# A gated decoder layer on one core: weights' low parts on VectorE, channel means in other banks, a new order of the gate jobs

## The chip, the cores and the metric

The kernel runs on one core of a Trainium2 chip. The metric is the device time of one execution in microseconds; the time given for a kernel is the median of its runs. One more execution was taken by the hardware profiler, and all rows below are from it.

## The reference

One decoder layer on a sequence of 1024 tokens and 1024 channels, in float32. With h the RMS-normalized input, one projection gives the parts of three branches and their gates:

```python
(c_glu, c_gate, d_q, d_k, d_v, d_gate, x_q, x_gate, merge) = split(h @ w_in)
# A: u = a * sigmoid(b); causal depthwise conv (k = 31) + bias; LayerNorm over channels; silu; * silu(c_gate); @ w_conv_proj
# B: differential attention, 8 heads of 2 x 64, ALiBi, RMS-normalized q and k; * silu(d_gate); @ w_diff_proj
# C: attention into 256 memory tokens, 4 heads of 256; * silu(x_gate); @ w_x_proj
g = sigmoid(merge)
x = x + (g[0] * y_conv + g[1] * y_diff + g[2] * y_mem) @ w_out
```

The LayerNorm of branch A needs the mean and the variance of the convolution's output over all 1024 channels. The kernel has channels on partitions, so these are sums over eight channel blocks and, in each, over the 128 partitions.

## The kernel before

**Numbers as two parts.** A matrix product in full precision is made of three matmuls of reduced-precision float32: each operand x is cut into a high part H (a cast on ScalarE) and a low part L = x - H (a subtraction on VectorE or GpSimd). `split` (L82) does both.

**Stages.** First the memory tokens, the norm of x, the first half of the GLU and the cross attention. Then, from L558 on, the Quads stage, which the change edits: the rest of the projection of h. Then the differential attention with the branch projections woven in, and last the output projection.

**Quads jobs.** In the Quads stage two blocks of 128 output channels are one job. A job is a two-by-two Strassen-like product (`strassen`, L629): seven products p1 to p7 of 12 matmuls each (128x128 weights, 512 moving columns), so 84 matmuls. The right-hand sides are quarters of h (tiles `hH`, `hL`) and the sums T1 to T4 of them, which `sums` (L580) makes once, at the start of the stage: for each of four k, GpSimd adds H and L of three quarters into tiles (`whole`, L572), VectorE subtracts these from each other, and `split` cuts the results. The left-hand sides are sums of quarters of the weights: `Quads.__call__` (L603) loads four raw tiles (two with tag "wraw", two with tag "wraw2" of 4 slots), GpSimd makes four sums of them (L621; s1 and s2 go to tag "ws" of 2 slots), ScalarE casts seven high parts (L623), and seven low parts follow (L624), some on GpSimd (`on_pool`) and the others on VectorE. The weights of a job are asked for in the middle of the job before.

The products of a job run into three accumulator banks, "tp" (tag a), "mm" (b) and "sc" (d). ScalarE copies a bank out between the products that it gathers (`snap`, L647, the "snap" of the text), VectorE adds (L650). The products p7, p3 and p4 of one job alternate with p1, p5 and p6 of the next, and with two "tp" banks the first product of a job needs the last snap of the bank two jobs back, which is taken only one product (2.7 us) earlier.

**The 38 jobs, in order:** 0 and 1 GLU, 2 to 5 merge gates, 6 and 7 GLU, 8 to 13 merge gates, 14 to 17 the cross-attention gate (`gx_out`, L740), then plain jobs (their output is only an activation and a store: the attention gate and v), and the convolution's gate (`gc_out`, L838); from job 28 on query/key jobs (`qk_out`, L755) with two more v jobs. While jobs 0 to 15 run, VectorE has the depthwise convolution to do (`conv`, L414, low priority: 31 instructions for each half block).

**The statistics.** `part_stats` (L802) brings each finished block back from memory and updates a running mean and deviation for each partition. After job 17 (MU_AT) `colmean` (L927) averages the mean over the 128 partitions by two matmuls with a matrix of 1/1024 for each half of the sequence (L931); after job 19 (RS_AT) the same for the deviation, followed by the chain `rstd_of` (L167: Ln, Exp and a Newton step) in place. `colsplit` (L919) cuts the operands one job earlier. `gate_in` (L818) later loads each block again and normalizes it: a - mean (L833), times dev (L834), Silu (L836).

**Order.** Only TensorE's order is that of the program. On the other engines and on SP, which issues all the DMAs, a scheduler with a timeline of its own orders the instructions by priority and estimated readiness; each engine then works in that order, and an instruction that waits holds all behind it. Tiles of one tag share its slots: a new tile waits until the one that had its slot is done with.

Of the kernel before, what the change touches and what calls it, by code (L numbers as in the profile page):

```python
# [10 lines left out]
F32R = mybir.dt.float32r  # L11
# [4 lines left out]
P = 128  # L16
S = 1024
# [13 lines left out]
def hybrid_layer(  # L31
# [36 lines left out]
    def new(pool, shape, tag, dt=F32, bufs=None):  # L68
        return pool.tile(shape, dt, tag=tag, name=tag, bufs=bufs)

    def r2f(ap):
        return ap.bitcast(F32)

    def mm_bank(tag="mm"):
        return banks[tag].tile([P, 512], F32, tag=tag, name=tag)
# [6 lines left out]
    def split(H, L, src):  # L82
        nc.scalar.copy(H, src)  # L83
        nc.vector.tensor_tensor(L, src, r2f(H), op=ALU.subtract)  # L84
# [5 lines left out]
    class Weights:  # L90


        def __init__(self, rows, width=512, low=None, high=None, ks=range(KK)):
            self.ks = ks
            self.raw = lambda kk: new(wp, [P, 512], "wraw", bufs=4)
            self.high = high or (lambda kk: nc.scalar.copy)
            self.rows, self.width, self.low, self.slices = rows, width, low or (lambda kk: nc.vector), None
# [106 lines left out]
    def halves():  # L204
        return [(half, slice(half * 512, half * 512 + 512)) for half in range(2)]
# [22 lines left out]
    with ExitStack() as st:  # L228
# [145 lines left out]
        for n in range(8):  # L374
# [10 lines left out]
            u = (m_u[1] if n == 0 else []) + x_u[n]  # L385
# [16 lines left out]
    cvp = cvs.enter_context(tc.tile_pool(name="cvp", bufs=2, side="right", reuse_waits="tile"))  # L402
    with ExitStack() as st:
        bp = st.enter_context(tc.tile_pool(name="bp", bufs=2, reuse_waits="tile"))
# [153 lines left out]
    with ExitStack() as st:  # L558
        bp = st.enter_context(tc.tile_pool(name="b2", bufs=2, reuse_waits="tile"))
# [12 lines left out]
        def whole(q, k, tag, bufs):  # L572
            t = new(bp, [P, 512], tag, bufs=bufs)
            H, L = quad[q](k)
            nc.gpsimd.tensor_tensor(t, r2f(H), r2f(L), op=ALU.add)
            return t
# [2 lines left out]

        def sums():  # L580
            for k in range(4):
                b11, b12 = whole("B11", k, "wraw2", 4), whole("B12", k, "wraw2", 4)
                b22 = whole("B22", k, "wraw2", 4)
                nc.vector.tensor_tensor(b11, b12, b11, op=ALU.subtract)
                split(*quad["T1"](k), b11)
                nc.vector.tensor_tensor(b12, b22, b12, op=ALU.subtract)
                split(*quad["T3"](k), b12)
                nc.vector.tensor_tensor(b22, b22, b11, op=ALU.subtract)
                split(*quad["T2"](k), b22)
                t4.append(whole("B21", k, "w4", 4))  # L590
                nc.vector.tensor_tensor(t4[k], t4[k], b22, op=ALU.subtract)
# [5 lines left out]
        class Quads:  # L597


            def __init__(self, c1, c2):  # L600
                self.c, self.ops, self.busy = (c1, c2), None, False

            def __call__(self):  # L603
                if self.ops is None:
                    raw = []
                    for i in range(2):
                        for j in range(2):
                            t = new(wp, [P, 512], "wraw", bufs=4) if i == 0 else new(bp, [P, 512], "wraw2", bufs=4)
                            c = self.c[i]
                            nc.sync.dma_start(t.rearrange("p (k c) -> p k c", k=4),  # L610
                                              w0[j * 512:j * 512 + 512, c:c + P].rearrange("(k p) c -> p k c", p=P))
                            raw.append(t)
                    a11, a12, a21, a22 = raw
                    s1, s2 = [new(bp, [P, 512], "ws", bufs=2) for _ in range(2)]
                    sums = {0: ((s1, a21, a22, ALU.add), (s2, s1, a11, ALU.subtract), (a21, a11, a21, ALU.subtract)),
                            6: ((a12, a12, s2, ALU.subtract),)}
                    on_pool = (1, 3, 4, 5, 6) if self.busy else (1, 3, 4, 6)
                    ops = {}
                    for n, a in ((0, a11), (1, s1), (2, s2), (3, a12), (4, a21), (6, a22), (5, a12)):
                        for o, x, y, op in sums.get(n, ()):  # L620
                            nc.gpsimd.tensor_tensor(o, x, y, op=op)  # L621
                        H, L = new(wp, [P, 512], "wH", F32R), new(wp, [P, 512], "wL", F32R)
                        nc.scalar.copy(H, a)  # L623
                        (nc.gpsimd if n in on_pool else nc.vector).tensor_tensor(L, a, r2f(H), op=ALU.subtract)  # L624
                        ops[n] = H, L
                    self.ops = [ops[n] for n in range(7)]
                return self.ops
# [162 lines left out]
        def spill(n, dst, c0, func=AF.Sigmoid):  # L790
            return [(Quads(c0 + n * 512 + p * 256, c0 + n * 512 + p * 256 + P), spill_out(dst, n * 512 + p * 256, func))
                    for p in range(2)]

        def glus(c2):
            return [(Quads(c2 * 256 + p * P, D + c2 * 256 + p * P), glu_out(2 * c2 + p)) for p in range(2)]
# [42 lines left out]
        def gc_out(c):  # L838
# [12 lines left out]
            return f  # L851

        sums()
        jobs = glus(2) + spill(2, sgT, C_MERGE) + spill(3, sgT, C_MERGE) + glus(3)
        for n in (4, 5, 1):
            jobs += spill(n, sgT, C_MERGE)
        def v_job(v):
            c = C_Q + 2 * D + v * 256
            return Quads(c, c + P), spill_out(vT[v], 0, None)
# [3 lines left out]
        def start(n, at, f):  # L863
            starts.setdefault((n, at), []).append(f)

        plain = spill(0, gdT, C_DGATE, AF.Silu) + spill(1, gdT, C_DGATE, AF.Silu) + [v_job(0), v_job(1)]
        for c in range(0, KK, 2):
            n = len(jobs)
            for (i, j), late, at in (((0, 0), 0, 3), ((1, 1), 0, 5), ((0, 1), 1, 0), ((1, 0), 1, 2)):
                start(n + late, at, gx_in(c + i, j))  # L870
            jobs.append((Quads(C_XGATE + c * P, C_XGATE + c * P + P), gx_out(c)))
        jobs += plain[:3]
        for c in range(0, KK, 2):
            for at, (i, j) in enumerate(((0, 0), (1, 1), (0, 1), (1, 0))):
                start(len(jobs) - 1, at, gate_in(c + i, j))
            jobs.append((Quads(C_GATE + c * P, C_GATE + c * P + P), gc_out(c)))
            jobs += plain[3:4]
            del plain[3:4]
        V_AT = {4: [2], 7: [3]}
        for h in range(DH):  # L880
            jobs.append((Quads(C_Q + h * P, C_Q + D + h * P), qk_out(h), True))
# [5 lines left out]
        def stats(n):  # L887

            if n == 1:
                nc.vector.memset(r2f(ones), 1.0 / D)  # L890
                nc.sync.dma_start(mean, cvT[0:P, :])
            if n in (MU_AT - 1, RS_AT - 1):
                with tc.issue_after(last[0].ins):
                    stat["cs"] = colsplit(mean if n < MU_AT else dev)
            if n == MU_AT:
                for half, sl in halves():
                    ps = colmean(half)
                    d = new(bp, [P, 512], "w4", bufs=4)
                    nc.vector.scalar_tensor_tensor(d, ps, -8.0, mean[:, sl], op0=ALU.mult, op1=ALU.add)
                    nc.scalar.activation(mean[:, sl], ps, AF.Copy, scale=8.0)  # L900
                    nc.scalar.activation(d, d, AF.Square, scale=math.sqrt(8.0))
                    nc.vector.tensor_tensor(dev[:, sl], dev[:, sl], d, op=ALU.add)
            if n == RS_AT:
                for half, sl in halves():
                    nc.scalar.copy(dev[:, sl], colmean(half))
                tc.keep_in_program_order(nc.scalar.preload_act_table_set(NLE))
                for half, sl in halves():
                    rstd_of(dev[:, sl], dev[:, sl], [P, 512], 1.0, 1e-5, eps5, nc.vector, bp, ("w4", "w4"), 4)
# [8 lines left out]
                on[:] = [f for f in on if next(f, 0) is None]  # L917

        def colsplit(src):  # L919
            cs = []  # L920
            for half, sl in halves():
                H, L = new(bp, [P, 512], "w4", F32R, bufs=4), new(bp, [P, 512], "w4", F32R, bufs=4)
                split(H, L, src[:, sl])
                cs.append((H, L))
            return cs

        def colmean(half):  # L927

            ps = mm_bank()
            for n, x in enumerate(stat["cs"][half]):  # L930
                nc.tensor.matmul(ps, lhsT=ones, rhs=x, start=n == 0, stop=n == 1)  # L931
            return ps
# [9 lines left out]

        gx, gc = g_load(gxT), g_load((gcH, gcL))
        due, AFTER, last, qkp = [], 1, [None], []
        for Q, *_ in jobs[2:16]:
            Q.busy = True
        PRE, MU_AT, RS_AT = 2, 17, 19
        weave(merge(0, bp, "sx", 7, AF.Sigmoid), pre(jobs[0][0]))
        sums4()
# [32 lines left out]
    with ExitStack() as st:  # L982
# [344 lines left out]
        c = 0  # L1327
# [47 lines left out]
    with ExitStack() as st:  # L1375
# [18 lines left out]
        for ci in range(2):  # L1394
            for db in range(4):
                if db == 1:
                    Ws[ci + 1]()
                d = 4 * ci + db
# [12 lines left out]
        for ci in range(2):  # L1411
            for sb in range(NS):
                if ci == 0 and sb == 2:
                    Wp["o"][1]()
                sl = slice(sb * P, sb * P + P)
# [37 lines left out]
```

## Time and profile before

| | |
|---|---|
| time of the runs, median (lowest to highest) | 1743.38 us (1742.48 to 1743.82) |
| the profiled execution: time | 1747.11 us |
| the profiled execution: span from first to last instruction | 1745.1 us |
| busy TensorE, VectorE, ScalarE, GpSimd | 95%, 74%, 53%, 53% of the span |
| mean granted TensorE clock | 0.978 |

PE is TensorE's matmuls, PEld its weight loads, DVE VectorE, ACT ScalarE, POOL GpSimd, SP the DMA queue's engine. Times in rows are us from the span's start, unless ns is said. An arrow in square brackets names what ended an engine's idle time. The clock is a share of 2.4 GHz; 0.5 is 1.2 GHz.

### The profile page before, as it was taken

Reading aid. Unit: us, or ns where it says so; the run is one execution under the profiler, and the core shown is the slowest. Engines: PE = TensorE matmul, PEld = TensorE weight load, DVE = VectorE, ACT = ScalarE, POOL = GpSimd, SP = SyncE. Lnnn points to the kernel's source line nnn. Section 1 sums busy time; section 2 is a strip of 40 time slices with the busy share of each in tenths; the row PEclk is TensorE's granted clock in tenths of the full one; section 3 lists DMA queues with packets and bytes.
Section 4 is the critical chain, followed back from the end, with each engine's and each line's share of the span. In section 5 each row is a group of like instructions: output and inputs, shape, how many; then the busy total and the mean of one; then the engine's idle time right before and its main releaser. Section 6 shows DMA issues by size and latency. Waiting matters only on the chain. (4 is left out here: it accounts for less than half of the span.)

```text
span 1745.1 us, 24253 instructions
## 1 busy us (share of the span) xinstructions
PE 1653.5 (95%) x7882; PEld 1371.4 (79%) x7882; DVE 1285.8 (74%) x2156; ACT 919.0 (53%) x1949; POOL 925.1 (53%) x935
## 2 busy tenths in 40 slices
PE   6999999989999999798999999998997999999999
PEld 5788888868887887677888778876886878877787
DVE  7979997998999998675664896744666677675911
ACT  5614645334544444465555786843676776763200
POOL 3220111678686876555665677544456564457820
PEclk8999999989999999899999999999998999999999
DMA  7410212232432445543444333297478455466632
GB/s 264 153 36 22 77 62 76 97 103 85 133 116 90 135 145 168 174 152 108 163 160 144 97 97 109 93 334 213 135 234 262 130 167 166 140 224 202 202 115 91
DMA packets 201399, 247.51 MB, mean 142 GB/s; under 512 B 15377, under 2 KB 109590, under 8 KB 201272
## 3 DMA queue, kind: packets, MB, share of 16 engines
q1 hardware_dynamic: 201272, 245.96, 43.6%
q8 instruction: 62, 1.02, 0.2%
q14 instruction: 65, 0.53, 0.1%
HBM read 172.50 MB, written 73.40 MB: 141 GB/s over the span
## 5 line engine op out<-in xcount | busy, mean ns | idle before, releaser
L422 DVE SCALAR_TENSOR_TENSOR cv<-u,cw,cv 128x512 f32<-128x512 f32 x464 | 348.9, 752 | 10.8
L113 POOL TENSOR_TENSOR wL<-wraw,wH 128x512 fp32r<-128x512 f32 x104 | 143.0, 1390 | 255.5 <-ACT wH L112 154.8
L78 PE MATMUL mm<-hH,wH 128*128 128x512 f32 x512 | 207.6, 406 | 0.6 <-DVE sg L1194 0.6
L624 POOL TENSOR_TENSOR wL<-wraw,wH 128x512 fp32r<-128x512 f32 x128 | 185.0, 1453 | 43.3 <-ACT wH L623 37.3
L80 PE MATMUL mm<-hH,wL 128*128 128x512 f32 x512 | 202.7, 396 | 0.0
L79 PE MATMUL mm<-hL,wH 128*128 128x512 f32 x512 | 202.6, 396 | 0.0
L623 ACT CAST wH<-wraw 128x512 fp32r<-128x512 f32 x190 | 115.2, 617 | 105.7 <-PE tp L642 37.7
L1054 DVE CUSTOM_DVE_ANT_0 p<-sc,dist 128x512 f32<-128x512 f32 (+3 forms) x192 | 100.3, 551 | 59.9 <-PE sc L1050 59.5
L642 PE MATMUL tp<-hH,wH 128*128 128x512 f32 x304 | 122.3, 402 | 17.1 <-ACT sx L647 17.1
L624 POOL TENSOR_TENSOR wL<-ws,wH 128x512 fp32r<-128x512 f32 x38 | 51.9, 1366 | 148.7 <-ACT wH L623 141.3
L1068 ACT ACTIVATE p<-p,nm 128x768 f32<-128x768 f32 (+7 forms) x128 | 98.3, 770 | 50.0 <-DVE nm L1066 49.7
L642 PE MATMUL tp<-hL,wH 128*128 128x512 f32 x304 | 121.5, 400 | 0.0
L642 PE MATMUL tp<-hH,wL 128*128 128x512 f32 x304 | 121.4, 399 | 0.0
L80 PEld LDWEIGHTS mm<-hH,wL 128*128 128x128 f32 x512 | 97.8, 191 | 21.5
L78 PEld LDWEIGHTS mm<-hH,wH 128*128 128x128 f32 x512 | 97.9, 191 | 18.6 <-DVE sg L1194 0.8
L79 PEld LDWEIGHTS mm<-hL,wH 128*128 128x128 f32 x512 | 98.1, 192 | 17.9
L112 ACT CAST wH<-wraw 128x512 fp32r<-128x512 f32 (+1 forms) x112 | 64.5, 589 | 64.1 <-PE mm L80 33.8
L647 ACT COPY sx<-tp 128x512 f32<-128x512 f32 x152 | 88.1, 579 | 12.3 <-PE tp L642 7.1
L623 ACT CAST wH<-ws 128x512 fp32r<-128x512 f32 x76 | 47.0, 619 | 73.5 <-PE tp L642 66.9
L642 PEld LDWEIGHTS tp<-hH,wH 128*128 128x128 f32 x304 | 59.0, 194 | 32.0 <-ACT sx L647 19.7
L1048 PE MATMUL sc<-k,q 128*128 128x512 f32 (+2 forms) x192 | 70.4, 374 | 10.8 <-DVE mx L1054 10.7
L1100 PEld LDWEIGHTS av<-v,a 128*128 128x128 f32 x576 | 70.5, 191 | 9.0 <-ACT a L1094 4.0
(319 smaller groups left out, 4812.6 us busy)
## 6 DMA issues: line engine op xcount, KB each, us to landing
wraw<-in_w_in_dram SPq DMA_DIRECT2D x184, 256.0 KB, 3.3
sg<-sgT SPq DMA_DIRECT2D x65, 256.0 KB, 3.4
sgT<-sx SPq DMA_DIRECT2D x48, 256.0 KB, 3.2
qf<-qT SPq DMA_DIRECT2D x32, 256.0 KB, 4.3
kf<-kT SPq DMA_DIRECT2D x32, 256.0 KB, 4.2
yT<-sg SPq DMA_DIRECT2D x32, 256.0 KB, 3.7
w<-cvT SPq DMA_DIRECT2D x20, 256.0 KB, 2.9
mw<-in_w_mem_kv_dram SPq DMA_DIRECT2D x16, 256.0 KB, 5.7
```

Source lines behind the costliest of these rows:

```text
L78: nc.tensor.matmul(ps, lhsT=lh, rhs=rh, start=start, stop=False)
L79: nc.tensor.matmul(ps, lhsT=lh, rhs=rl, start=False, stop=False)
L80: nc.tensor.matmul(ps, lhsT=ll, rhs=rh, start=False, stop=stop)
L113: self.low(kk).tensor_tensor(L[:, :w], raw[:, :w], r2f(H[:, :w]), op=ALU.subtract)
L422: nc.vector.scalar_tensor_tensor(ps if j < CONV_K - 1 else acc, u[:, at - j:at - j + 512], cw[:, c, 30 - j:31 - j], ps, op0=ALU.mult, op1= ...
L623: nc.scalar.copy(H, a)
L624: (nc.gpsimd if n in on_pool else nc.vector).tensor_tensor(L, a, r2f(H), op=ALU.subtract)
L642: nc.tensor.matmul(R[bank], lhsT=l[:, ks], rhs=r, start=start and k == 0 and i == 0, stop=stop and k == 3 and i == 2, skip_group_check=True)
L647: last[0] = nc.scalar.copy(R[n], R[bank])
L1054: nc.vector.tensor_tensor_reduce(out=pm[m][:, k0:k0 + w], in0=sc[m][:, :w], in1=dist[:, d0:d0 + w], scale=1.0, scalar=-3.0e38, op0=ALU.add ...
L1068: nc.scalar.activation(pm[m][:, :n], pm[m][:, :n], AF.Exp, bias=nm[:, m:m + 1], scale=slope, accum_out=sm[:, m:m + 1])
L1100: nc.tensor.matmul(A["av"][:, t * P:t * P + P], lhsT=A["a", jp][:, c * P:c * P + P], rhs=T["v", j // 4][:, j % 4, :], start=j == 0 and t = ...
```

## The change

Five edits, all in the Quads stage. (1) The set of low parts that go to GpSimd: as before in jobs 0 and 1 (four) and 2 to 15 (five), but none from job 16 on, where it was four; all seven are then VectorE's. (2) In `sums`, b11 and b12 are tiles of tag "ws" in place of "wraw2". (3) `colmean` uses banks "av" and "cv" for the two halves in place of "mm" twice. (4) `colsplit` puts its parts into two full-length tiles of tag "u" (two slots, those of the convolution's input) in place of four of tag "w4" (four slots); one scratch tile of the statistics moves from "w4" to "acc". (5) Four of the plain jobs stand ahead of the first conv-gate job, where it was three. The order of jobs 18 on is then plain x 4, conv gate 0, v, conv gate 2, v, conv gate 4, conv gate 6; it was plain x 3, conv gate 0, plain, conv gate 2, v, conv gate 4, v, conv gate 6.

```diff
@@ sums
-                b11, b12 = whole("B11", k, "wraw2", 4), whole("B12", k, "wraw2", 4)
+                b11, b12 = whole("B11", k, "ws", 2), whole("B12", k, "ws", 2)
@@ Quads
-                self.c, self.ops, self.busy = (c1, c2), None, False
+                self.c, self.ops, self.stage = (c1, c2), None, "gates"
-                    on_pool = (1, 3, 4, 5, 6) if self.busy else (1, 3, 4, 6)
+                    on_pool = {"start": (1, 3, 4, 6), "conv": (1, 3, 4, 5, 6), "gates": ()}[self.stage]
@@ jobs
-        jobs += plain[:3]
+        jobs += plain[:4]
         for c in range(0, KK, 2):
...
             jobs.append((Quads(C_GATE + c * P, C_GATE + c * P + P), gc_out(c)))
-            jobs += plain[3:4]
-            del plain[3:4]
+            jobs += plain[4 + c // 2:5 + c // 2]
@@ stats
-                    d = new(bp, [P, 512], "w4", bufs=4)
+                    d = new(cvp, [P, 512], "acc")
@@
         def colsplit(src):
-            cs = []
+            H, L = [new(cvp, [P, S], "u").bitcast(F32R) for _ in range(2)]
             for half, sl in halves():
-                H, L = new(bp, [P, 512], "w4", F32R, bufs=4), new(bp, [P, 512], "w4", F32R, bufs=4)
-                split(H, L, src[:, sl])
-                cs.append((H, L))
-            return cs
+                split(H[:, sl], L[:, sl], src[:, sl])
+            return [(H[:, sl], L[:, sl]) for _, sl in halves()]
         def colmean(half):
-            ps = mm_bank()
+            ps = mm_bank(("av", "cv")[half])
@@
-        for Q, *_ in jobs[2:16]:
-            Q.busy = True
+        for n, (Q, *_) in enumerate(jobs[:16]):
+            Q.stage = "start" if n < 2 else "conv"
```

## Rows read from the trace of the kernel before

**Rows 1.** TensorE's waits, whole run: for whom, us in total, times, longest

```profile
PE tp L642 <- ACT sx L647: 24.8, 8, 6.5
...
PE mm L931 <- DVE sx L650: 5.9, 2, 5.3
...
PE av L773 <- DVE ms L84: 2.6, 4, 0.7
```

**Rows 2.** Windows cut at job starts: jobs 3, 16 to 21, 24, 31

```profile
core 0: us, PE busy (x) PEld busy (x) DVE busy (x) ACT busy (x) POOL busy (x), PEclk, DMA share, GB/s
424.00:443.00 19.00, 19.00 (x85) 15.76 (x84) 18.61 (x24) 9.48 (x17) 13.36 (x11) 1.00 0.40 125
...
676.90:702.80 25.90, 19.37 (x85) 15.71 (x85) 18.72 (x17) 11.84 (x23) 19.09 (x13) 0.97 0.68 223
702.80:731.30 28.50, 23.18 (x89) 18.67 (x90) 17.61 (x18) 12.64 (x24) 12.76 (x9) 0.86 0.44 144
731.30:753.40 22.10, 21.05 (x85) 16.89 (x83) 17.82 (x20) 11.81 (x22) 12.93 (x8) 0.91 0.54 186
753.40:774.40 21.00, 20.39 (x89) 16.57 (x90) 14.26 (x16) 12.52 (x24) 12.07 (x8) 1.00 0.44 149
774.40:799.30 24.90, 19.22 (x86) 15.58 (x84) 20.50 (x24) 18.31 (x27) 12.28 (x8) 0.95 0.35 113
799.30:820.40 21.10, 21.10 (x84) 17.30 (x85) 6.89 (x9) 10.77 (x19) 10.28 (x8) 0.90 0.42 132
...
858.50:877.60 19.10, 19.10 (x86) 15.81 (x85) 14.43 (x16) 11.95 (x21) 13.77 (x9) 1.00 0.55 181
...
998.90:1020.80 21.90, 21.26 (x93) 17.15 (x92) 19.91 (x21) 17.69 (x33) 15.86 (x10) 1.00 0.30 96
```

**Rows 3.** TensorE's timeline: the first matmul after each of four waits

```profile
377.46 0.79 PE L642 MATMUL tp<-T2H,wH 128*128 128x512 f32 x1 [6.34 <-ACT sx L647]
...
702.78 0.79 PE L642 MATMUL tp<-hH,wH 128*128 128x512 f32 x1 [6.48 <-ACT sx L647]
...
730.28 1.19 PE L931 MATMUL mm<-w,ones 128*128 128x512 f32 x2 [5.32 <-DVE sx L650]
...
799.28 0.79 PE L642 MATMUL tp<-hH,wH 128*128 128x512 f32 x1 [5.68 <-ACT sx L647]
```

**Rows 4.** ScalarE's timeline near the same waits

```profile
375.26 1.14 ACT L623 CAST wH<-wraw 128x512 fp32r<-128x512 f32 x2 [4.45 <-POOL wraw L621]
...
712.16 0.62 ACT L83 CAST w<-mean 128x512 fp32r<-128x512 f32 x1 [7.87 <-DMA gxTL<-w]
...
724.16 0.62 ACT L83 CAST w<-mean 128x512 fp32r<-128x512 f32 x1 [3.17 <-DMA gxTL<-w]
...
791.81 0.63 ACT L728 ACTIVATE sx<-sx 128x512 f32<-128x512 f32 x1 [3.61 <-DVE sx L650]
```

**Rows 5.** VectorE's timeline, jobs 16 to 20

```profile
690.51 1.76 DVE L811 SCALAR_TENSOR_TENSOR mean<-acc,mean 128x512 f32<-128x512 f32 x1 [3.30 <-POOL acc L809]
692.20 1.77 DVE L624 TENSOR_TENSOR wL<-ws,wH 128x512 fp32r<-128x512 f32 x1
...
728.14 0.79 DVE L84 TENSOR_TENSOR w<-mean,w 128x512 fp32r<-128x512 f32 x1 [2.12 <-DMA gxTL<-w]
728.85 0.68 DVE L624 TENSOR_TENSOR wL<-wraw,wH 128x512 fp32r<-128x512 f32 x1
729.45 0.68 DVE L650 TENSOR_TENSOR sx<-mm,sx 128x512 f32<-128x512 f32 x1
...
787.69 1.78 DVE L833 TENSOR_TENSOR w<-w,mean 128x512 f32<-128x512 f32 x1
```

**Rows 6.** GpSimd's timeline: first job sum of job 0; a low part

```profile
362.88 1.29 POOL L621 TENSOR_TENSOR ws<-wraw,wraw 128x512 f32<-128x512 f32 x1 [7.58 <-DMA sgT<-sx]
...
713.38 1.29 POOL L624 TENSOR_TENSOR wL<-ws,wH 128x512 fp32r<-128x512 f32 x1 [9.78 <-ACT wH L623]
```

**Rows 7.** GpSimd's groups, 676.9 to 1146: xcount | busy us, mean ns | idle before

```profile
L624 POOL TENSOR_TENSOR wL<-wraw,wH 128x512 fp32r<-128x512 f32 x64 | 98.3, 1544 | 26.9 <-ACT wH L623 20.9 <-DVE u L833 3.0 <-PE av L773 1.3
```

**Rows 8.** SP's timeline: the two loads into "wraw2" for job 0

```profile
355.87 4.14 SPq L610 DMA_DIRECT2D wraw<-in_w_in_dram  x2
```

## The prediction

> **What bounds the kernel now.** The order in which I read: the waits of TensorE over the whole run, then the windows cut at the job boundaries, then the instructions of each engine around the waits that the windows point to. TensorE's waits add up to little in the run, and the largest group is for the snap of an accumulator bank by ScalarE (L647), 24.8 us in 8 waits; two waits before the channel-mean matmuls L931 cost 5.9 us [rows 1]. In the windows the reader sees that an undisturbed Quads job (84 matmuls) takes 19.0 us, 0.226 us a matmul, with TensorE busy all of it, and that this holds even where VectorE is 98% busy with the convolution (18.61 of 19.00 us, the window at 424). So VectorE's load alone doesn't hold TensorE; a snap that stands behind a blocked instruction does. Jobs 16 to 21 (676.9 to 820.4) are longer by 6.9, 9.5, 3.1, 2.0, 5.9 and 2.1 us [rows 2]. That is 29.5 us; the eight matmuls L931 are 1.8 of it, which leaves 27.7 us of waits and of lower clock after them. I split it into five stalls by the waits [rows 3] and the granted clock [rows 2] (job 21 has no wait of its own, but a clock of 0.90, and is 2.1 us long for it, so this is the price of the 1.2 GHz level after a long stall):
>
> A, ending 702.78: 6.9 us in job 16 and some 2.5 us of low clock after it, 9.4 us. B, before the second half of the mean's L931, ending 730.28: 5.3 us, 0.8 us of low clock in job 17 and 2.0 us in job 18 (0.09 of 22.1 us), 8.1 us. C, the rest of job 18: 1.1 us. D, the second pair of L931 in job 19: 2.0 - 0.9 = 1.1 us. E, ending 799.28: 5.9 us in job 20 and 2.1 us in job 21, 8.0 us.
>
> One more stall lies in job 0: 6.3 us up to 377.46 [rows 3], and with as much low clock after it as after A about 9 us. The query/key jobs (one is the window at 998.9) take 21.9 us: 19.0, eight matmuls of the means (1.8) and 1.1 us that contains a wait for VectorE's low part L84 (2.6 us in four such waits) [rows 1, 2].
>
> **The change part by part.**
>
> *Channel means.* B is a wait for bank "mm": VectorE reads it at 729.45 for 0.68 us (L650), and TensorE goes on at 730.28 [rows 3, 5]. In banks "av" and "cv", unused at that time, this wait goes. But the bank isn't all: the low part of the same mean (L84) ran only at 728.14, 2.12 us late for a DMA that empties a "w4" tile, and ScalarE stood at its L83 for 7.87 and 3.17 us for the same reason [rows 4, 5]. The new bank alone would move the matmul from 730.28 to about 729.0, 1.3 us. Since the four "w4" tiles go too (the "u" slots are free: the convolution's last output was written before), both causes fall. The snap of the job before, behind that L83, comes earlier by the 3.17 us. I take 7.5 of B's 8.1 us, bounds 1.3 and 8.1. D has the same cause; I take 1.0. The price: gate_in's first "u" tiles now come after the second L931 (about 774), no longer long ahead. Their four loads queue on SP behind that release, and VectorE's L833 and L834 behind the loads. They are due one job after that, so I count nothing; without this cover it is one load and two subtractions, some 5 us.
>
> *Order of jobs.* Moving the fourth plain gate job ahead puts gate_in for conv channels 0 and 1 one job (19 us) behind the rstd chain of job 20, no longer beside it. E is the snap held behind the Silu at 791.81, which waited 3.61 us for VectorE's add L650, which stood behind L833 (787.69, 1.78 us) and its neighbours of the same length, the rstd product and a low part [rows 4, 5]. Without the two to four gate_in instructions there (3 to 7 us) most of E goes; the table switches of the chain stay. I take 5 of 8.0, bounds 0 and 8.0. C lies behind the same hoisted L833: 1.0, bounds 0 and 1.1. Every other DMA keeps its job; the last two gate jobs now follow each other. The heaviest gate window had 14.43 of 19.1 us on VectorE (at 858.5) [rows 2], so room is left: 0, bound a loss of 6 (1 us a job).
>
> *Low parts on VectorE.* In 22 jobs four TensorTensors move from GpSimd (1544 ns in the mean of the larger group) [rows 7] to VectorE. One takes 1.29 us there undisturbed (713.38) [rows 6]. On VectorE a low part takes 0.68 us when alone (728.85) and 1.77 while GpSimd works (692.20) [rows 5]. In a query/key job VectorE has 21 instructions and 19.9 busy us of 21.9, GpSimd ten [rows 2]. At 0.68 each the 21 need 14.3 us, so ten GpSimd instructions cost VectorE 5.6 us of waiting, 0.56 each. After: 25 x 0.68 + 6 x 0.56 = 20.4 us against 19.9. It still fits. I take 1 us gained in all, as the 1.1 us wait may shrink a little; bounds: at 1.77 each the four cost 7.1 us against 2.0 us of room, 5 us lost in each of six full jobs, 30; or the wait goes in all six, 6 gained. Queued behind a low part on VectorE that waits for ScalarE's cast are the adds L650, behind these the Silu on ScalarE, and behind that the snap. On GpSimd the first low part of a job waited 9.78 us for its cast at 713.38 [rows 6] and nobody minded.
>
> The Trainium skill, "SBUF — State Buffer", section "Who interferes with whom", has it that a VectorE instruction with two SBUF inputs and a GpSimd instruction that reads SBUF exclude each other for the whole of the first one. By this rule, with 1.29 and 0.68 us, six GpSimd instructions and 18 of VectorE that read two SBUF operands hold the port for 20.0 us of a query/key job, against 22.4 for ten and 14 before, and the sum would have 6 us here in place of 1. The trace agrees in kind (1.77 beside 0.68), but it shows waits of 0.56 us, not 1.29, for each GpSimd instruction.
>
> A is not touched by name: VectorE waited 3.30 us for GpSimd's L809 at 690.51 and then worked off a row of instructions of about 1.77 us [rows 5], ScalarE and the snap behind it. Fewer low parts on GpSimd shorten it, more on VectorE lengthen it: 0, bounds a gain of 9.4 and a loss of 4.
>
> *Sums at the start (L582).* With b11 and b12 in "ws", the second matrix's raw tiles no longer wait for the end of the sums. Now their second load is issued near 359.6, as the last subtraction of the sums ends, and GpSimd's first job sum starts at 362.88, 7.58 us idle; ScalarE's cast at 375.26 waits for a later one of these, and the snap behind it for the cast [rows 4, 6, 8]. After, the first sum needs only "ws", free at about 359.7: 3 us earlier. The two-slot "ws" lets b11 and b12 of a step start after the last one's, two GpSimd instructions as b12 and b22 are now, so the pace stays. I take 3 gained; bounds 9 gained, 2 lost.
>
> Sum: 7.5 + 1 + 5 + 1 + 1 + 3 = 18.5 us off a span of 1745.1. That execution took 1747.1 with what lies around the span, 3.7 above the median of 1743.4; the difference is carried over to the median: **1725 us**.
>
> **The rivals.**
>
> *R1, the stalls move.* The bank waits go, but the mean and rstd chains still end late, and TensorE meets ScalarE's late snap one job on. For: the snap waits (24.8 us) are four times those of the banks; the table switches stay. Against: undisturbed gate jobs of 19.0 us. Gain: 1.3 to 3 of B, 1 of D, 3 at the start: 1737.
>
> *R2, VectorE's queue becomes the bound (slower).* A moved low part blocks the in-order queue in the query/key jobs, where 2.0 us are free. For: the 91% there. Against: 98% under the convolution with no loss. At the upper bound 30 us are lost: 1743.4 - 18.5 + 30 = 1755. It decides above 2.3 us a job over the eight jobs. The Trainium skill, "Perfetto Trace Analysis", section "Optimizing Scalar/DVE Operations", advises moving work off a saturated VectorE, and adds that between it and GpSimd this might not help because they share a read port. The change goes the other way, and no row of this trace yet shows which half of that advice holds here.
>
> *R3, GpSimd's quiet also takes A and the query/key waits.* For: the row of 1.77 us instructions behind A. Against: its first cause is a load, not GpSimd. 18.5 + 9.4 x 0.8 + 5 = 31: 1712.
>
> **How the numbers follow.** The forecast has 0.53 (its own range 1717 to 1733), R1 0.20, R2 0.14, R3 0.13. About 0.2%, 3.5 us, is what a measurement can tell from no change: 1739.9 to 1746.9. R1 reaches it with 0.07 of its 0.20, R2 with 0.02 of its 0.14. Faster: 0.53 + 0.13 + 0.13 = 0.79; same 0.09; slower 0.12. A range from 1711 to 1743 leaves out R2, the far end of R1 and the lower part of R3, 0.2 together.
>
> **What would show it.** L931 in other banks with no wait over 1 us; jobs 17 to 20 at 19 to 21 us with the clock at 2.4 GHz; first job sum near 359.7; VectorE's low parts mostly at 0.68 us; query/key jobs no longer than 21.9. Wrong: query/key jobs over 24 us, a snap wait over 4 us in jobs 17 to 21, or VectorE idle behind casts while ScalarE waits for its adds.

## The result and the profile after

The changed kernel takes 1715.9 us in the median of four runs (1714.7 to 1723.8), the kernel before beside it 1743.6 us (1742.5 to 1748.3). The ratio is 0.985, with a 95% interval from 0.982 to 0.987: 27.7 us faster, where 18.5 were forecast (1725 us, range 1711 to 1743). The profiled execution took 1714.70 us with a span of 1712.9 us and a mean clock of 0.988. The changed source is three lines shorter from `colmean` on, so L931 of before is L928 now, and in the attention L1048 is L1045.

TensorE's waits, whole run, as in [rows 1]:

```profile
PE tp L642 <- ACT sx L647: 5.7, 4, 2.7
PE tp L642 <- DVE wL L624: 5.6, 2, 3.0
PE sc L642 <- POOL wL L624: 3.2, 1, 3.2
PE av L773 <- DVE ms L84: 1.8, 4, 0.5
```

The waits for the snap fell from 24.8 to 5.7 us, those at the channel means are gone. In their place are three waits for low parts, 8.8 us, all in jobs 0 and 1. The windows, cut at job starts as in [rows 2]: job 1, jobs 16 to 21, a gate job (24), a query/key job (31):

```profile
core 0: us, PE busy (x) PEld busy (x) DVE busy (x) ACT busy (x) POOL busy (x), PEclk, DMA share, GB/s
...
384.10:407.80 23.70, 20.73 (x85) 16.73 (x84) 21.35 (x21) 10.12 (x18) 23.07 (x17) 0.93 0.26 78
...
678.40:697.80 19.40, 19.38 (x85) 15.69 (x84) 19.30 (x21) 11.86 (x22) 11.47 (x8) 1.00 0.67 217
697.80:717.90 20.10, 20.08 (x88) 16.64 (x89) 19.88 (x26) 13.76 (x25) 10.38 (x5) 1.00 0.67 211
717.90:737.00 19.10, 19.10 (x86) 15.80 (x85) 17.04 (x22) 13.23 (x25) 6.61 (x4) 1.00 0.76 251
737.00:756.90 19.90, 19.90 (x89) 16.50 (x88) 11.39 (x16) 10.73 (x20) 5.50 (x4) 1.00 0.55 177
756.90:776.30 19.40, 19.29 (x86) 15.62 (x85) 16.38 (x25) 15.96 (x25) 7.60 (x4) 1.00 0.48 151
776.30:795.40 19.10, 19.10 (x84) 15.84 (x85) 16.04 (x22) 11.67 (x21) 7.92 (x5) 1.00 0.51 164
852.60:871.60 19.00, 19.00 (x85) 15.74 (x84) 14.10 (x18) 12.34 (x22) 5.82 (x4) 1.00 0.57 179
...
972.00:993.70 21.70, 21.24 (x93) 17.17 (x92) 20.21 (x25) 17.59 (x33) 9.56 (x6) 1.00 0.30 97
```

Read the lengths first: jobs 16 to 21 take 117.0 us where they took 143.5, and the clock stays at 2.4 GHz. VectorE does 25 instructions in the query/key job in place of 21, in 20.2 busy us in place of 19.9; GpSimd's part falls from 15.9 to 9.6 us. In jobs 16 and 17 VectorE is 99% busy, and TensorE waits for next to nothing.

Where the 32.2 us between the two spans went: jobs 15 to 21 give 27.1, jobs 28 to 36 give 2.6, jobs 0 and 1 lose 2.7, job 37 loses 2.1 (it takes 32.0 to 36.4 us over all these kernels, for reasons not looked for), the jobs between give 0.7, and 6.7 lie behind the last matmul of the Quads stage, where nothing was changed. That tail took 578 to 583 us in all twelve profiles of the experiments below, also where only the sums or only the banks were edited, against 586.8 in the one profile of before. So most of these 6.7 us belong to that execution and not to the change; the medians, 27.7 us apart, lie near the 25.6 that the Quads stage gave.

VectorE's timeline at the place of stall A, to be read beside [rows 5]:

```profile
686.37 0.68 DVE L811 SCALAR_TENSOR_TENSOR mean<-acc,mean 128x512 f32<-128x512 f32 x1
...
689.88 1.77 DVE L624 TENSOR_TENSOR wL<-ws,wH 128x512 fp32r<-128x512 f32 x1
691.58 0.68 DVE L650 TENSOR_TENSOR sx<-sx 128x512 f32<-128x512 f32 x1
692.19 0.68 DVE L84 TENSOR_TENSOR w<-w,sx 128x512 fp32r<-128x512 f32 x1
```

The instruction that updates the mean took 1.76 us with 3.30 us of idling before it; it takes 0.68 now, without idling. A row of five instructions of 1.77 us has become a mixture of 0.68 and 1.77. ScalarE's Silu behind VectorE's add waits less for it, before and after:

```profile
695.71 0.63 ACT L744 ACTIVATE sx<-sx 128x512 f32<-128x512 f32 x1 [7.10 <-DVE sx L650]
...
692.29 0.63 ACT L744 ACTIVATE sx<-sx 128x512 f32<-128x512 f32 x1 [2.38 <-DVE sx L650]
```

The channel means, on TensorE's timeline, run back to back in their two banks, with no wait, where 5.32 us stood in [rows 3]:

```profile
717.00 0.63 PE L928 MATMUL av<-u,ones 128*128 128x512 f32 x2
717.46 0.63 PE L928 MATMUL cv<-u,ones 128*128 128x512 f32 x2
```

And the start, which lost: GpSimd's sums (b11 and b12 of the second step, b11 of the third, the first job sum), SP's two loads into "wraw2", and TensorE's three waits.

```profile
336.94 3.44 POOL L575 TENSOR_TENSOR ws<-hH,hL 128x512 f32<-128x512 f32 x2
347.76 1.29 POOL L575 TENSOR_TENSOR ws<-hH,hL 128x512 f32<-128x512 f32 x1 [7.38 <-DVE wraw L588]
...
365.08 1.30 POOL L621 TENSOR_TENSOR ws<-wraw,wraw 128x512 f32<-128x512 f32 x1 [5.07 <-DVE wraw L588]
```

```profile
339.25 0.38 SPq L610 DMA_DIRECT2D wraw<-in_w_in_dram  x1
...
351.92 0.38 SPq L610 DMA_DIRECT2D wraw<-in_w_in_dram  x1
```

```profile
372.08 0.50 PE L642 MATMUL sc<-T1H,wL 128*128 128x512 f32 x1 [3.25 <-POOL wL L624]
377.69 0.79 PE L642 MATMUL tp<-T2H,wL 128*128 128x512 f32 x1 [2.60 <-DVE wL L624]
387.71 0.79 PE L642 MATMUL tp<-hH,wL 128*128 128x512 f32 x1 [2.97 <-DVE wL L624]
```

The loads come 16.6 and about 8 us earlier, as foreseen, but the first job sum starts at 365.08 and not at 359.7.

### The profile page after: what moved, and what is told of

Same layout as the page of the kernel before. It is cut to its first block, busy times and chain, and to the rows that moved or that the text cites. A ratio compares the mean times of both kernels' runs of the same rounds, so it can differ in the third digit from the quotient of the medians.

```text
span 1712.9 us, 24246 instructions
## 1 busy us (share of the span) xinstructions
PE 1642.1 (96%) x7882; PEld 1362.9 (80%) x7882; DVE 1306.7 (76%) x2244; ACT 917.5 (54%) x1948; POOL 801.3 (47%) x847
## 5 line engine op out<-in xcount | busy, mean ns | idle before, releaser
L113 POOL TENSOR_TENSOR wL<-wraw,wH 128x512 fp32r<-128x512 f32 x104 | 144.1, 1400 | 257.0 <-ACT wH L112 159.7
L621 POOL TENSOR_TENSOR ws<-wraw,wraw 128x512 f32<-128x512 f32 x38 | 60.9, 1604 | 188.7 <-DVE wL L624 118.7
L624 DVE TENSOR_TENSOR wL<-wraw,wH 128x512 fp32r<-128x512 f32 x128 | 107.7, 847 | 19.2 <-ACT wH L623 19.0
L624 POOL TENSOR_TENSOR wL<-wraw,wH 128x512 fp32r<-128x512 f32 x62 | 85.0, 1377 | 13.7 <-ACT wH L623 13.6
L621 POOL TENSOR_TENSOR wraw<-wraw,ws 128x512 f32<-128x512 f32 x38 | 59.6, 1567 | 51.8 <-DVE wL L624 50.1
L1045 PE MATMUL sc<-k,q 128*128 128x512 f32 (+2 forms) x192 | 69.8, 371 | 10.5 <-DVE mx L1051 10.3
```

The lines of the kernel that those rows point to most:

```text
L113: self.low(kk).tensor_tensor(L[:, :w], raw[:, :w], r2f(H[:, :w]), op=ALU.subtract)
```

## The experiments

Two theories of the stalls in jobs 15 to 21 stood against each other. P: the low parts on GpSimd make VectorE's instructions long, ScalarE waits for VectorE, and the snap behind ScalarE. S: the channel means, by their "w4" tiles and bank "mm", hold ScalarE and VectorE up, and the rest follows. Each of the change's parts was done alone, then taken out of the whole, and two of them were turned round. The table has the length of stretches, from the first matmul of a job to that of another, in the profile of each kernel; the ratio is to the kernel before in runs beside it (1741.5 to 1743.6 us in the median), with its 95% interval. Where intervals overlap, as those of changed, no_order, no_sums and qk_pool do, the stretches tell the kernels apart: each is from one execution, but jobs 0 and 1 take 38.0 to 39.8 us in all nine kernels with the old sums and 41.3 to 42.5 in all five with the new.

| kernel | jobs 0-1 | jobs 15-21 | jobs 28-36 | median us | ratio (interval) |
|---|---|---|---|---|---|
| before | 39.6 | 163.3 | 191.3 | 1743.6 | 1 |
| changed | 42.3 | 136.2 | 188.7 | 1715.9 | 0.985 (0.982 to 0.987) |
| lows_only | 38.0 | 146.5 | 188.7 | 1720.2 | 0.988 (0.985 to 0.990) |
| means_only | 38.2 | 150.9 | 191.1 | 1729.0 | 0.992 (0.990 to 0.995) |
| order_only | 39.7 | 156.4 | 191.2 | 1738.2 | 0.998 (0.996 to 1.000) |
| sums_only | 41.3 | 166.0 | 191.1 | 1744.4 | 1.002 (1.001 to 1.004) |
| banks_only | 39.8 | 163.1 | 191.3 | 1743.8 | 0.999 (0.997 to 1.000) |
| tiles_only | 39.6 | 152.9 | 191.3 | 1732.3 | 0.992 (0.989 to 0.995) |
| no_lows | 41.4 | 144.9 | 191.3 | 1730.2 | 0.991 (0.988 to 0.994) |
| no_order | 41.4 | 136.8 | 188.6 | 1712.2 | 0.983 (0.981 to 0.984) |
| no_sums | 38.2 | 136.4 | 188.7 | 1711.2 | 0.982 (0.980 to 0.984) |
| lows_means | 39.7 | 136.6 | 188.6 | 1709.0 | 0.978 (0.975 to 0.982) |
| qk_pool | 42.5 | 136.1 | 192.9 | 1718.9 | 0.987 (0.985 to 0.989) |
| all_pool | 39.3 | 165.0 | 196.5 | 1754.7 | 1.007 (1.005 to 1.009) |

With no stall jobs 15 to 21 would take 7 x 19.04 + 1.8 = 135.1 us.

### One part alone

**lows_only**: the kernel before with the first part of the diff.

```diff
-                    on_pool = (1, 3, 4, 5, 6) if self.busy else (1, 3, 4, 6)
+                    on_pool = {"start": (1, 3, 4, 6), "conv": (1, 3, 4, 5, 6), "gates": ()}[self.stage]
```

> The kernel before with the low parts alone changed (none on GpSimd from job 16 on). Theory P (GpSimd's low parts hold VectorE at the shared port, ScalarE waits behind VectorE, the snap behind ScalarE): stalls A and most of E go, jobs 16, 20 and 21 come near 19 us, query/key jobs to 21.8; B stays with a wait of 4 to 6 us at L931; 1720 to 1728 us. Theory S (stalls come from the w4 tiles and the mm bank of the channel means): A and E stay within 2 us, 1738 to 1743 us.

1720.2 us. TensorE's waits in jobs 16 and 17:

```profile
694.81 0.50 PE L642 MATMUL tp<-hH,wH 128*128 128x512 f32 x1 [1.78 <-ACT sx L647]
...
719.89 1.19 PE L931 MATMUL mm<-w,ones 128*128 128x512 f32 x2 [4.98 <-DVE sx L650]
```

A's wait fell from 6.48 to 1.78 us, and the clock was 1.00 in the 19.1 us after it. VectorE still idles 2.79 us for GpSimd's L809 there, but of the row of five long instructions only the first, L811 (1.75 us), is left. Job 20 took 19.09 us and job 21 19.05, so E is gone; B stayed. This is P's forecast in each point but job 16, which takes 21.11 us and not 19.

One rival of P is that GpSimd's low parts come too late for TensorE or ScalarE. The trace of before has no such wait: from job 15 to job 21 ScalarE waits for VectorE, TensorE and DMAs, never for GpSimd, and TensorE for no low part of the weights.

**means_only**: the kernel before with the banks, the "u" tiles and the "acc" tile.

```diff
-                H, L = new(bp, [P, 512], "w4", F32R, bufs=4), new(bp, [P, 512], "w4", F32R, bufs=4)
+            H, L = [new(cvp, [P, S], "u").bitcast(F32R) for _ in range(2)]
-            ps = mm_bank()
+            ps = mm_bank(("av", "cv")[half])
```

> The kernel before with the channel means alone changed (banks av and cv, tiles u and acc). Theory P: only B, C and D go, 8 to 10 us, A and E stay: 1732 to 1737 us. Theory S: A to E all go, 25 us or more: at most 1720 us.

1729.0 us, beyond P's forecast and short of S's. TensorE, then ScalarE and VectorE at what is left of E:

```profile
698.50 0.80 PE L642 MATMUL tp<-hH,wH 128*128 128x512 f32 x1 [3.51 <-ACT sx L647]
...
785.71 0.80 PE L642 MATMUL tp<-hH,wH 128*128 128x512 f32 x1 [6.16 <-ACT sx L647]
```

```profile
783.85 0.82 ACT L836 ACTIVATE u<-u,cw 128x512 f32<-128x512 f32 x1 [2.11 <-DVE u L834]
```

```profile
782.07 3.42 DVE L834 TENSOR_TENSOR u<-u,dev 128x512 f32<-128x512 f32 x2
```

B, C and D went, and with them half of A: 3.51 us are left of its 6.48. So A had two causes, and S holds for one of them. SP's loads, before and then in means_only, and GpSimd's L809 in the same order, show how the tiles act:

```profile
675.40 0.91 SPq L830 DMA_DIRECT2D u<-cvT  x2
...
684.40 0.32 SPq L806 DMA_DIRECT2D acc<-cvT  x1
...
678.15 0.32 SPq L806 DMA_DIRECT2D acc<-cvT  x1
```

```profile
689.20 1.29 POOL L809 TENSOR_TENSOR acc<-acc,mean 128x512 f32<-128x512 f32 x1 [3.74 <-DMA wraw<-in_w_in_dram]
...
681.43 1.64 POOL L809 TENSOR_TENSOR acc<-acc,mean 128x512 f32<-128x512 f32 x1 [1.98 <-DMA acc<-cvT]
```

Before, SP issues two of gate_in's loads into "u" (L830) and then, 7.5 us after the first matmul of job 16, the load of the last statistics block (L806). With the "u" tiles taken by the means no L830 stands there, and L806 comes 2.5 us after that matmul. (That the profile ends L809's wait before with a load of weights, which L809 does not read, means little: in lows_only, where L809 is as late, it names the load of "acc".) VectorE's idling for L809 falls from 3.30 to 0.59 us. It is 0.60 in tiles_only too, but 3.42 in banks_only and 2.79 in lows_only. The other half of A, the row of 1.77 us, stays.

E stayed whole: the Silu L836 of gate_in waits for two L834 that take 3.42 us beside GpSimd, and the snap stands behind the Silu.

**banks_only** and **tiles_only** take that part in two: the line of `colmean` alone, and the lines of `colsplit` and the scratch tile alone.

> The kernel before with banks av and cv for the channel means, nothing else. The prediction gave the bank alone 1.3 us of B, since the low part of the mean waits for a w4 tile until 728.1 anyway: the second L931 still waits 3 us or more, jobs 17 and 18 stay over 49 us together (50.7 before), 1739 to 1743 us. Rival: the bank is all of it, jobs 17 and 18 fall to about 43, 1734 us.

> The kernel before with the channel means' parts in u and acc tiles, the bank mm as before. By the prediction the w4 wait delays ScalarE and VectorE and so also the bank's reader: most of B goes without new banks, jobs 17 and 18 at 42 to 45 us, 1733 to 1738 us. Rival: without new banks B stays, 1739 to 1744 us.

1743.8 and 1732.3 us. TensorE at the mean's matmuls, with the new banks alone:

```profile
726.99 0.50 PE L931 MATMUL cv<-w,ones 128*128 128x512 f32 x1 [0.26 <-ACT w L83]
731.15 0.80 PE L931 MATMUL cv<-w,ones 128*128 128x512 f32 x1 [3.65 <-DVE w L84]
```

and with the new tiles alone:

```profile
722.74 0.72 PE L929 MATMUL mm<-u,ones 128*128 128x512 f32 x2 [0.74 <-DVE sx L650]
```

With the banks alone the same wait has a new name: it now ends with the low part of the mean, which waits for a "w4" tile. The tiles are the cause, the bank is what ended last in the trace of before.

**order_only**: `jobs += plain[:4]` and its second line, nothing else.

> The kernel before with the fourth plain gate job moved ahead, nothing else. Both theories leave A and B (8 us each). If gate_in beside the rstd chain makes E, E goes: 1735 to 1739 us; if VectorE's and GpSimd's contention makes it, E stays: 1742 to 1745 us.

1738.2 us. E's wait fell from 5.68 to 2.02 us, and job 21 behind it ran at a clock of 1.00 (19.19 us); A and B stayed, with waits of 5.79 and 4.42 us.

**sums_only**: the line of `sums`, nothing else.

> The kernel before with b11 and b12 of the start's sums in ws, nothing else. By the prediction job 0 shortens by 3 us: 1740 us. By the changed kernel's jobs 0 and 1 (18.6 and 23.7 us against 20.5 and 19.0) it is a loss of some 3 us: 1746 us.

1744.4 us, a ratio of 1.002. Jobs 0 and 1 are 1.7 us longer in the profile, and jobs 15 to 21 another 2.7, for which no cause was looked for.

### One part taken out or turned round

**no_order** and **no_sums** are the changed kernel with the old order, and with the old tiles in `sums`.

> The changed kernel with the order of gate jobs of before. Theory P (the port is what made E): the low parts alone already take E, so job 20 stays near 19 us and the time within 1.5 us of the changed kernel's, 1715 to 1718. Theory O (gate_in beside the rstd chain makes E): 5 to 8 us come back in jobs 20 and 21, 1721 to 1724 us.

> The changed kernel with b11 and b12 of the start's sums back in wraw2. If the two-slot ws costs what sums_only and the first two jobs show (1.7 to 2.7 us there), jobs 0 and 1 fall from 42.3 to 38 to 40 us and the time is 2 to 4 us under the changed kernel's, about 1712 us. If that was chance of the scheduler, it is within 1 us of it.

1712.2 us without the order: the changed kernel is not slower for losing it, and job 20 takes 19.78 us against 19.32. 1711.2 us without the sums' edit: jobs 0 and 1 fall by 4.1 us to 38.2.

**no_lows**: the changed kernel with `on_pool` as before.

> The changed kernel with the low parts as before (four on GpSimd from job 16 on). Theory P: half of A stays (22.8 and 22.8 us in jobs 16 and 17 as with the means alone), query/key jobs as before (191 us for jobs 28 to 37 against 188.7): 1724 to 1729 us. Rival: the other parts suffice, as the order did in the changed kernel: 1715 to 1718 us.

1730.2 us. A wait of 3.39 us is left of A and one of 3.42 us of E (with the order in, otherwise 6.16), and the query/key jobs are as long as before.

**qk_pool**: the changed kernel, with GpSimd's four low parts back in jobs 28 to 37.

```diff
-        for n, (Q, *_) in enumerate(jobs[:16]):
-            Q.stage = "start" if n < 2 else "conv"
+        for n, (Q, *_) in enumerate(jobs):
+            Q.stage = "start" if n < 2 or n >= 28 else "conv" if n < 16 else "gates"
```

> The changed kernel with four low parts back on GpSimd in the query/key jobs 28 to 37 alone. Theory P: those jobs get as long as before, 29 to 33 at 23.1 and 21.9 us in place of 21.5 and 21.8: 2 to 3 us slower, 1718 us. Rival Q (VectorE's in-order queue is the worse place in these jobs): they get shorter than 21.8, 1713 us or less.

1718.9 us, not clear of the changed kernel's 1715.9 by the intervals; the stretch is, 192.9 us against 188.7. Job 29 takes 24.66 us in place of 21.47, jobs 30 to 33 about 22.0 in place of 21.77. In these jobs VectorE is the better place, though it is 93% busy.

**all_pool**: the kernel before, with all seven low parts of jobs 16 to 37 on GpSimd.

```diff
-                    on_pool = (1, 3, 4, 5, 6) if self.busy else (1, 3, 4, 6)
+                    on_pool = (1, 3, 4, 5, 6) if self.busy else (0, 1, 2, 3, 4, 5, 6) if self.late else (1, 3, 4, 6)
```

> The kernel before with all seven low parts of every job from 16 on placed on GpSimd, in place of four: the change's first part in the other direction. Theory P (each low part on GpSimd holds the port for 1.29 us, on VectorE for 0.68): the stalls in jobs 15 to 21 grow, 163 us there become 170 to 185, and query/key jobs pass 22 us: 1750 to 1775 us. Rival L (VectorE's number of instructions is what delays ScalarE): VectorE has three fewer a job, stalls shrink: 1725 to 1738 us.

1754.7 us. Windows of jobs 23 and 31:

```profile
842.80:865.90 23.10, 19.23 (x85) 15.58 (x83) 15.07 (x15) 9.55 (x19) 15.29 (x11) 1.00 0.47 158
1010.70:1033.40 22.70, 21.28 (x93) 17.19 (x92) 18.23 (x19) 17.59 (x33) 19.73 (x13) 1.00 0.30 93
```

VectorE has fewer instructions and is less busy (18.23 us against 19.91), and yet the query/key job is 0.8 us longer: the rival L falls. But P's size was too large: jobs 15 to 21 grew by 1.7 us only; 5.7 us came in jobs 23 and 24, where there was no stall before, and 5.2 in jobs 28 to 36. In job 23 a late load has a part as well: VectorE idles 5.69 us for gate_in's "u" before its row of long instructions.

**lows_means**: the two parts that are left, without the order and the sums' edit.

> The changed kernel without the sums' ws and without the new order: low parts and channel means alone. If the order adds nothing and ws costs 2 to 4 us, it is at 1708 to 1713 us, under the changed kernel; jobs 0 and 1 at 38 us together, jobs 15 to 21 at 136 to 137.

1709.0 us, the fastest. Its ratio lies under the changed kernel's, with intervals that just don't meet; no_sums and no_order lie between. Part of the lead is no gain of the omission: jobs 9 and 10 took 19.04 us each here, and all other kernels paid 2.8 to 4.7 us there, around a snap wait of 2.55 to 2.90. Why this one does not was not tried.

## Why the prediction held, point by point

The forecast was right in direction and range, and its picture of the kernel (a snap behind a blocked ScalarE behind VectorE) is what the experiments show. Of the signs that it named only the early first job sum failed to come. But 1715.9 us lies below the 1717 to 1733 that it gave the forecast itself, and it was made of terms that were off on both sides: the low parts, put at 1 us, were worth most, the order, put at 6, gave nothing in company, and the sums, put at 3, cost 2 to 4. That these errors partly cancel is luck. Nor do the terms add: the low parts alone shorten jobs 15 to 21 and 28 to 36 by 19.4 us (lows_only), and in company by 11.3 (no_lows against the changed kernel), since A and E can each be shortened by more than one part.

**Channel means: 7.5 + 1.0 forecast, right.** Jobs 17 to 19 are 8.0 us shorter in lows_means than in lows_only. B went with the tiles, and the bank alone was worth next to nothing, where the prediction gave it 1.3 us: the bank's small part and the "w4" wait behind it could be read in [rows 5]. It overlooked that the same tiles also made half of A: it saw that gate_in's loads would come later and looked there for a price only, not for the load L806 that goes ahead.

**Order: 5 + 1 forecast, nothing in company.** Alone the order takes 5.6 us of E (jobs 20 and 21 of order_only), near the 5 forecast, but by another way. The step that failed is that moving the job would take gate_in's work on VectorE away from the rstd chain. In order_only L834 and L833 still stand in job 20, from 785.97 on, and in the changed kernel L833 does, at 760.56: the scheduler pulls them forward. What left job 20 of order_only is the Silu L836, behind which the last snap of E stood in the kernel before:

```profile
797.43 0.81 ACT L836 ACTIVATE u<-u,cw 128x512 f32<-128x512 f32 x1 [2.85 <-DVE u L834]
```

The prediction named the Silu at 791.81 instead. The second step that failed is that E would be there for the order alone: with the low parts on VectorE none of it is left to take, as lows_only and no_order show. C, put at 1.0 with the order, did not go with it: the wait of 1.10 us before job 19 is 0.75 in order_only and gone in lows_only and means_only.

**Low parts: 1 forecast, some 14 measured** (no_lows against the changed kernel by the medians), of which 2.6 in the query/key jobs and 8.7 in jobs 15 to 21: 4.8 at A (jobs 16 and 17) and 3.3 at E (job 20). E was not counted here at all. A was put at 0 with a bound of 9.4, and this is the step that was mis-sized: low parts gone from GpSimd were set against low parts added on VectorE as if they weighed the same. The prediction had the numbers that say they don't, 1.29 us against 0.68, and used them for the query/key jobs only. There it forecast 20.4 busy us for VectorE, and 20.2 were measured. The rule of the Trainium skill that it set beside this ("SBUF — State Buffer", "Who interferes with whom") gave 6 us for the query/key jobs; measured were 2.6, between the rule's sum and the row's.

**Sums: 3 gained forecast, 2 to 4 lost.** The loads came early, as foreseen, and the pace of the steps nearly stayed (8.67 us between two L588, 8.45 and 8.01 before). What failed is the step "GpSimd's first job sum at about 359.7". With all four "wraw2" slots free for b22, the scheduler put the b22 sums and the other four (L575 into "w4") ahead of the second step's b11, which stood at 327.08 before and stands at 336.94 now. The later steps are 4.5 to 5.4 us late for it, and the two-slot "ws" makes the first job sum wait for their end. The prediction looked for the price in the tiles' waits and not in what the freed tiles let go ahead.

**The rivals.** R3, where A and the query/key waits go too, is nearest to what happened: A went, and half of the 5 us in the query/key jobs came (2.6), but the start and order terms that it also counted did not. R2, VectorE's queue as the bound, did not occur: it was 93% busy in query/key jobs and 99% in jobs 16 and 17 with no loss. The count of jobs behind R2 was loose (six full ones in the bound, eight in the threshold): five, 29 to 33, took 21.9 us or more before. Of the advice that the prediction quoted from the Trainium skill ("Perfetto Trace Analysis", "Optimizing Scalar/DVE Operations"), qk_pool and all_pool bear out the second half: giving work to GpSimd was no relief for VectorE. R1 is out, as stalls C to E did not move on: jobs 22 to 28 took 19.04 us each.

What stays open: how much of A each cause holds at the level of single instructions (lows_only leaves 1.78 us of 6.48, means_only 3.51; together they leave nothing), why SP's order has L806 late beside gate_in's loads, and why jobs 9 and 10 lose their stall in one kernel.

## What to carry to other kernels

Before an instruction is given to GpSimd, compare how long each engine keeps the other out, not how busy they are: here VectorE at 99% with short instructions (jobs 16 and 17) was better than at 72% and 62% with long ones. Where a wait ends with one resource, look for the next that would end it (banks_only moved the wait's name from the bank to the tile) before it is counted as gained. And where a scheduler orders the engines, freeing tiles or moving a job changes what is pulled forward: each part of a change is worth a run of its own, since here the order and the sums' edit were worth nothing or less in company.

## What the runs showed of the hardware

GpSimd, too, can be kept out for long. One sum L621 took 4.59 us in the changed kernel while VectorE had eight instructions behind each other from 704.09 to 708.98, each of 0.68 us and 0.60 us apart; it was done 1.2 us after the last. GpSimd's timeline, and the first and the last of VectorE's eight:

```profile
705.56 4.59 POOL L621 TENSOR_TENSOR ws<-wraw,wraw 128x512 f32<-128x512 f32 x1 [6.92 <-DMA wraw<-in_w_in_dram]
710.23 1.63 POOL L621 TENSOR_TENSOR wraw<-wraw,wraw 128x512 f32<-128x512 f32 x1
```

```profile
704.09 0.68 DVE L624 TENSOR_TENSOR wL<-ws,wH 128x512 fp32r<-128x512 f32 x1
...
708.30 0.68 DVE L747 TENSOR_TENSOR w<-w,sx 128x512 f32<-128x512 f32 x1
```

It is not the only one: in the changed kernel two more GpSimd instructions took 3.22 and 2.83 us (at 771.86 and 785.88), and in means_only one took 4.42:

```profile
777.19 4.42 POOL L624 TENSOR_TENSOR wL<-wraw,wH 128x512 fp32r<-128x512 f32 x1 [3.35 <-DVE w L833]
```

Each ran beside VectorE instructions of 0.68 us without a gap, and each ended 1.1 to 1.2 us after the last of these that reads two tiles; an add L650 that reads an accumulator bank came next and ran beside it. In the row of stall A [rows 5] VectorE's instructions follow each other without a gap as well, but there each takes 1.77 us, and GpSimd's 1.3 to 1.7. The difference that the rows show is who was first: at A GpSimd was at work when the row began, and in the four long cases VectorE was when GpSimd's instruction came. That this decides is a reading of these rows, which no run tested. In jobs 15 to 21 of the changed kernel neither TensorE nor ScalarE waited for GpSimd, so its long sums cost nothing.
